# Low halves of the weight blocks: an accumulating GpSimd DMA in place of a VectorE subtraction

## The chip, the cores and the metric

The kernel runs on one core of one Trainium2 chip. A core has a matrix engine (TensorE, PE in the profile), a vector engine (VectorE, DVE), an activation engine (ScalarE, ACT), a general engine (GpSimd, POOL) and a queue that issues plain transfers (SyncE, SP). The profile counts the loading of matmul weights apart, as PEld. Sixteen DMA engines move data for all queues. The metric is the device time of one execution in microseconds (us), the median of several runs. One execution has been recorded by the hardware profiler, and all rows of the trace come from it.

## The reference

The reference is one layer of a decoder trunk on 512 tokens of width 1024, with 16 learned tokens put in front (528 positions in all). Its steps:

```
u    = rmsnorm(h) * w
proj = u @ w_in                       # pool | z | x,B,C | dt | two gates
y_pool = pool_mixer(proj.pool) @ w_pool_up        # causal means over 2, 4, 8, 16 positions
xbc  = silu(causal_conv4(proj.xBC));  dt = softplus(proj.dt + dt_bias)
y    = ssd_chunked(x, dt, -exp(a_log), B, C) + x * d_skip   # Mamba-2, chunks of 128, 8 groups of 4 heads
y_ssd = (group_rmsnorm(y * silu(z)) * norm_w) @ w_ssd_out
h    = h + (gate_pool * y_pool + gate_ssd * y_ssd) @ w_o
h    = h + relu(rmsnorm(h) @ w_ff1)**2 @ w_ff2
out  = rmsnorm(h)[16:]
```

Everything is float32, and nearly all of the arithmetic is products with weight matrices.

## The kernel before, in words

**Products in three parts.** TensorE takes the operands in a rounded form of float32 (F32R in the code). To keep precision, every operand is split in two: a high half, which is the value rounded to that form, and a low half, which is the value minus its high half. A product is then three matmuls: high by high, high by low, low by high (`mm3`, lines 88 to 93, and `proj_step`, lines 139 to 146, where the low half of the weights is read by line 146).

**Weight blocks.** The host lays all weights out as blocks of 128 partitions by 1024 float32 (512 KB), in the order in which the program uses them. `block()` (lines 76 to 79) takes the next one: SP loads it into `raw` (line 72), ScalarE copies it, rounded, into `whi` (line 73), and VectorE subtracts the high half from the raw block and writes `wlo` (line 74). There are three buffers for `raw` and four each for `whi` and `wlo` (lines 66 to 68 and 55). A buffer of `whi` or `wlo` is free again when TensorE has read it for the last time. A block is 48 matmuls of some 260 columns, or 24 of 512.

**Stages.** The first stage works on the input as it arrives: the time-step weights, then eight blocks for group 0 and three gates (lines 520 to 525). Then comes a loop over the eight groups of the state-space part (line 562): `ssd(g)` does the group's own arithmetic on ScalarE, VectorE and TensorE, and is woven with `group_proj(g + 1)`, which runs the projections of the next group from four blocks `px`, at times one gate, and two blocks `pz`, and with parts of the output projection (`pso`, `psp`). Then come the pooling branch (`pp`, `psl`, `pg`), the gates and merge (`pgs`, `pup`), the output product (`wo`), and last the feed-forward part (`pf`).

**The feed-forward part.** It uses a recursive scheme (Strassen and Winograd) on quarters of the second weight matrix. In each of seven rounds, four blocks of the first matrix (`pf`, lines 867 to 887 and 911 to 944) are mixed with seven products of the second (`alpha`, `p`, `q`, lines 956 to 958). The operands of the latter are sums of quarters, made by GpSimd (line 967, 128x1024 each) and then split by ScalarE and VectorE (`split`, lines 713 to 719, into the same four buffers of `whi` and `wlo`, where the profile calls them `shi` and `slo`).

**What sets the order.** Each engine runs its instructions in one fixed order. That order is made when the program is built: a planner goes through the program with its own costs and, on each engine, takes what is ready by then, the earlier in the program first. On the chip an engine stops at an instruction whose operands are not there, and what is queued behind it waits as well. GpSimd is one such queue: it holds the loads of `abc` (line 391, one for each group, from a buffer in DRAM), of `ht` and `fw` (lines 754 and 755), and the sums of line 967.

Of the kernel before, what the change touches and what calls it, by code (L numbers as in the profile page):

```python
# [11 lines left out]
AF = mybir.ActivationFunctionType  # L12
ALU = mybir.AluOpType
# [36 lines left out]
def kernel(ctx: ExitStack, tc, xT, x, w, vec, fnw, out):  # L50
    nc = tc.nc
    act, dve, pe, pool = nc.scalar, nc.vector, nc.tensor, nc.gpsimd
# [6 lines left out]


    nblk = [0]

    def block_tiles():
        b = nblk[0]
        nblk[0] += 1
        return (b, wp.tile([P, 1024], F32, tag="raw", name=f"raw{b}", bufs=3),
                wp.tile([P, 1024], F32R, tag="whi", name=f"whi{b}"),
                wp.tile([P, 1024], F32R, tag="wlo", name=f"wlo{b}"))

    def block_part(t, c):  # L70
        b, raw, hi, lo = t
        nc.sync.dma_start(raw[:, c], w[b, :, c])
        act.copy(hi[:, c], raw[:, c])  # L73
        dve.tensor_tensor(lo[:, c], raw[:, c], hi[:, c].bitcast(F32), op=ALU.subtract)  # L74

    def block():
        t = block_tiles()
        block_part(t, slice(0, 1024))
        return t[2:]

    def units():

        while True:
            hi, lo = block()
            for j in range(NK):
                yield hi[:, j * P : (j + 1) * P], lo[:, j * P : (j + 1) * P]
# [94 lines left out]
    b, raw, hi, lo = wdt  # L181
# [156 lines left out]
    def group_tiles(g):  # L338
        xc = gc.tile([P, 2, L], F32, tag="xc", name=f"xc{g}")
        bt = gc.tile([P, L], F32, tag="bt", name=f"bt{g}")  # L340
        ct = gc.tile([P, SEQ], F32, tag="ct", name=f"ct{g}")
        zt = gc.tile([P, 2, SEQ], F32, tag="zt", name=f"zt{g}", bufs=1)
        return xc, bt, ct, zt
# [7 lines left out]
    def group_proj(g, cur, gate=None):  # L351

        first = g == 0
        xc, bt, ct, zt = cur
        for dst, t, skip in ((bt, 16 + g, 0), (ct, 24 + g, NM - 4), (xc[:, 0, :], 2 * g, 0),
                             (xc[:, 1, :], 2 * g + 1, 0)):
            if first and dst is bt:
                view = viewB
            else:
                runs, view = wide(psum2(f"px{g}_{t}"), skip)  # L360
                proj(runs, block(), X if first else U)
            conv(dst, first_raw(t, view, skip) if first else view, t)
            yield
        if gate is not None:
            gate_pool(gate)
            yield
        ps = psum2(f"pz{g}")
        for i in range(2):
            proj(narrow(ps[:, i * SEQ : (i + 1) * SEQ]), block(), X if first else U)
        zf = zt.rearrange("p i t -> p (i t)")  # L370
        if first:
            dve.tensor_tensor(zt, ps.rearrange("p (i t) -> p i t", i=2),
                              rsb[:, NM:].unsqueeze(1).to_broadcast([P, 2, SEQ]), op=ALU.mult)
            act.activation(zf, zf, AF.Silu)
        else:
            act.activation(zf, ps, AF.Silu)
        yield
# [125 lines left out]
    def weave(a, b, n):  # L503

        end = object()
        a = [a]
        while a or b:
            for s in [a] + [b] * n:
                if s and next(s[0], end) is end:
                    s.pop(0)  # L510
# [33 lines left out]
    def out_half():  # L544
        for dd in range(4):
            ps = psum2(f"pso{dd}")
            for i in range(2):
                ssd_out(2 * dd + i, ps[:, i * SEQ : (i + 1) * SEQ], range(8))
                act.copy(acc[2 * dd + i], ps[:, i * SEQ : (i + 1) * SEQ])
                yield  # L550

    def out_part():

        un = units()
        for d in range(NK):
            ps = psum2(f"psp{d}")[:, :SEQ]
            for k in range(8, 14):
                mm3(ps, next(un), ys[k], k == 8, k == 13)
            dve.tensor_tensor(acc[d], acc[d], ps, op=ALU.add)
            yield  # L560

    for g in range(G):
        nxt = group_tiles(g + 1) if g + 1 < G else None
        fill = [group_proj(g + 1, nxt, GATE_AT.get(g))] if nxt else [out_part()]
        if g == 4:
            fill = [out_half()] + fill
        weave(ssd(g, cur), fill, 2 if g == 4 else 1)
        cur = nxt
# [638 lines left out]
```

## Time and profile before

| | us |
|---|---|
| median of 2 runs | 1025.61 (1025.49 to 1025.72) |
| span of the profiled execution, first to last instruction | 1023.3 |
| what lies around the span, to the median | 2.3 |
| TensorE busy | 1014.6 |
| VectorE busy | 730.3 |
| ScalarE busy | 552.5 |
| GpSimd busy | 88.7 |

The time of the profiled execution itself is not given beside its span; the 2.3 us is the median less the span. Busy times are those of one engine and overlap. Issuing a DMA is not counted as busy for SP and ScalarE. Where a row of a group stands, its columns are the line, the engine, the operation with the tiles that it writes and reads, the shapes, the count, then busy time and the mean length of one in ns, then the idle time of that engine ahead of these instructions and what ended it. In a timeline, the columns are start, length, engine, line, operation, and in brackets the idle time before it.

### The profile page before, as it was taken

How to read it: one execution, taken by the hardware profiler on the slowest of the kernel's cores; microseconds unless marked ns; L12 is line 12 of the kernel's file. 1: busy time of each engine (PE TensorE's matmuls, PEld its weight loads, DVE VectorE, ACT ScalarE, POOL GpSimd, SP SyncE). 2: the span in 40 equal slices, each digit the busy share in tenths (PEclk: the TensorE clock that was granted, in tenths of full speed). 3: DMA queues.
4: the chain of work that ended last, by engine and by line, in shares of the span. 5: the costliest groups of instructions: out<-in, count | busy, mean ns of one | idle time of the engine just before them, and what ended most of it. 6: DMA issues, size and time to landing. Idle time of an engine off the chain costs nothing.

```text
span 1023.3 us, 14063 instructions
## 1 busy us (share of the span) xinstructions
PE 1014.6 (99%) x5697; PEld 876.7 (86%) x5697; DVE 730.3 (71%) x954; ACT 552.5 (54%) x728; POOL 88.7 (9%) x52
## 2 busy tenths in 40 slices
PE   9999999999999999999999999999999999999997
PEld 8889989998879898988899888888888888888886
DVE  7978788687746586978755457975777577666866
ACT  7775968586627339573244343474545355454444
POOL 0100000000000000000000001003040421413400
PEclk9999999999999999999999999999999999999999
DMA  7243051414332331414532333224323323334112
GB/s 237 72 160 103 21 166 38 148 46 141 102 101 86 103 104 42 145 41 141 189 102 84 103 104 120 86 91 156 103 69 122 120 83 113 95 102 124 42 42 83
DMA packets 29281, 105.63 MB, mean 103 GB/s; under 512 B 3296, under 2 KB 4256, under 8 KB 28192
## 3 DMA queue, kind: packets, MB, share of 16 engines
q1 hardware_dynamic: 26496, 92.75, 28.7%
q0 software_dynamic: 2000, 11.08, 3.0%
q8 instruction: 45, 0.74, 0.3%
q10 hardware_dynamic: 720, 0.91, 0.3%
q14 instruction: 20, 0.16, 0.1%
HBM read 102.55 MB, written 2.16 MB: 102 GB/s over the span
## 4 chain that ended last, share of the span: by engine, by line
PE 96%; DVE 2%; ACT 0%; DMA 0%; issue 0%; SPq 0%; ACTq 0%
PE px L143 6%; PE px L144 6%; PE pf L92 6%; PE pf L91 6%; PE px L146 6%; PE pf L90 6%; PE alpha L956 3%; PE alpha L957 3%; PE alpha L958 3%; PE pz L143 3%; PE pz L146 3%; PE pz L144 3%; PE py L470 2%; PE pso L90 2%; PE pp L144 2%; PE pp L146 2%
## 5 line engine op out<-in xcount | busy, mean ns | idle before, releaser
L73 ACT CAST whi<-raw 128x1024 fp32r<-128x1024 f32 (+1 forms) x131 | 135.7, 1043 | 220.0 <-PE pf L91 55.8
L74 DVE TENSOR_TENSOR wlo<-raw,whi 128x1024 fp32r<-128x1024 f32 (+1 forms) x131 | 163.6, 1251 | 112.6 <-ACT whi L73 105.3
L143 PE MATMUL px<-uh,whi 128*128 128x264 f32 (+1 forms) x448 | 121.2, 290 | 0.7 <-DVE ct L334 0.7
L144 PE MATMUL px<-ul,whi 128*128 128x264 f32 (+1 forms) x448 | 118.9, 285 | 0.0
L90 PE MATMUL pf<-vh,whi 128*128 128x512 f32 x256 | 99.8, 390 | 0.0
L92 PE MATMUL pf<-vh,wlo 128*128 128x512 f32 x256 | 99.6, 389 | 0.0
L91 PE MATMUL pf<-vl,whi 128*128 128x512 f32 x256 | 99.6, 389 | 0.0
L146 PE MATMUL px<-uh,wlo 128*128 128x264 f32 (+1 forms) x448 | 90.8, 284 | 0.0
L143 PEld LDWEIGHTS px<-uh,whi 128*128 128x128 f32 x448 | 84.6, 189 | 2.8 <-issue 2.6
L144 PEld LDWEIGHTS px<-ul,whi 128*128 128x128 f32 x448 | 84.8, 189 | 0.3
L718 DVE TENSOR_TENSOR slo<-b,shi 128x1024 fp32r<-128x1024 f32 x35 | 49.1, 1403 | 31.6 <-ACT shi L717 31.6
L146 PEld LDWEIGHTS px<-uh,wlo 128*128 128x128 f32 x448 | 69.4, 188 | 0.3 <-issue 0.3
L717 ACT CAST shi<-b 128x1024 fp32r<-128x1024 f32 x35 | 36.8, 1050 | 47.2 <-PE pf L91 36.4
L91 PEld LDWEIGHTS pf<-vl,whi 128*128 128x128 f32 x256 | 48.1, 188 | 10.0
L90 PEld LDWEIGHTS pf<-vh,whi 128*128 128x128 f32 x256 | 48.1, 188 | 9.9
L92 PEld LDWEIGHTS pf<-vh,wlo 128*128 128x128 f32 x256 | 48.1, 188 | 9.9
L967 POOL TENSOR_TENSOR b<-b,b 128x1024 f32<-128x1024 f32 x14 | 35.7, 2548 | 238.3 <-DVE slo L718 238.3
L956 PE MATMUL alpha<-shi,hh 128*128 128x512 f32 x140 | 54.6, 390 | 0.0
L957 PE MATMUL alpha<-slo,hh 128*128 128x512 f32 x140 | 54.5, 389 | 0.0
L958 PE MATMUL alpha<-shi,hl 128*128 128x512 f32 x140 | 54.5, 389 | 0.0
L783 DVE TENSOR_TENSOR ht<-ht,alpha 128x1024 f32<-128x1024 f32 x35 | 42.5, 1214 | 10.9 <-PE alpha L958 10.9
L143 PE MATMUL pz<-uh,whi 128*128 128x512 f32 x112 | 44.0, 393 | 0.0
(412 smaller groups left out, 2513.7 us busy)
## 6 DMA issues: line engine op xcount, KB each, us to landing
raw<-in_w SPq DMA_DIRECT2D x129, 512.0 KB, 3.6
b<-in_w SPq DMA_DIRECT2D x28, 512.0 KB, 3.6
abc<-acs_d POOLq DMA_DIRECT2D x8, 1024.0 KB, 7.2
wob<-in_w SPq DMA_DIRECT2D x8, 512.0 KB, 4.6
xt<-in_xT SPq DMA_DIRECT2D x8, 264.0 KB, 5.6
ht<-in_x POOLq DMA_DIRECT2D x4, 512.0 KB, 6.7
w<-in_w SPq DMA_DIRECT2D x4, 512.0 KB, 3.6
out_dram<-out SPq DMA_DIRECT2D x4, 320.0 KB, 2.4
```

Of the source, the lines that this page charges most:

```text
L73: act.copy(hi[:, c], raw[:, c])
L74: dve.tensor_tensor(lo[:, c], raw[:, c], hi[:, c].bitcast(F32), op=ALU.subtract)
L90: pe.matmul(ps, ah, bh, start=first, stop=False)
L91: pe.matmul(ps, ah, bl, start=False, stop=False)
L92: pe.matmul(ps, al, bh, start=False, stop=last)
L143: pe.matmul(o, wh, rhs[0][k][:, c], start=k == 0, stop=False)
L144: pe.matmul(o, wh, rhs[1][k][:, c], start=False, stop=False)
L146: pe.matmul(o, wl, rhs[0][k][:, c], start=False, stop=k == NK - 1)
L718: dve.tensor_tensor(lo, src, hi.bitcast(F32), op=ALU.subtract)
L956: pe.matmul(ps[t], a[0], wh[:, cs], start=f, stop=False, skip_group_check=True)
L957: pe.matmul(ps[t], a[0], wl[:, cs], start=False, stop=False, skip_group_check=True)
L958: pe.matmul(ps[t], a[1], wh[:, cs], start=False, stop=l, skip_group_check=True)
```

## The change

From the loop over the groups on, a block's low half is made in another way. ScalarE writes the negated rounded block into `wlo` (its own scaling by -1 on the way), and a DMA that GpSimd issues reads the block from DRAM once more and adds it to what stands in `wlo`. ScalarE then makes the high half as before. The first-stage blocks, and all operands that go through `split`, stay as they were.

```
+    low_by_dma = [False]
...
     def block():
         t = block_tiles()
-        block_part(t, slice(0, 1024))
+        if not low_by_dma[0]:
+            block_part(t, slice(0, 1024))
+            return t[2:]
+        b, raw, hi, lo = t
+        nc.sync.dma_start(raw, w[b])
+        act.activation(lo, raw, AF.Copy, scale=-1.0)
+        nc.gpsimd.dma_start(lo, w[b], accum_op=ALU.add)
+        act.copy(hi, raw)
         return t[2:]
...
+    low_by_dma[0] = True
     for g in range(G):
         nxt = group_tiles(g + 1) if g + 1 < G else None
```

## The prediction

> **What bounds the kernel now.** First the page: busy times, then the engine shares of the chain that ended last.
>
> ```profile
> span 1023.3 us, 14063 instructions
> PE 1014.6 (99%) x5697; PEld 876.7 (86%) x5697; DVE 730.3 (71%) x954; ACT 552.5 (54%) x728; POOL 88.7 (9%) x52
> ...
> PE 96%; DVE 2%; ACT 0%; DMA 0%; issue 0%; SPq 0%; ACTq 0%
> ```
>
> TensorE is busy for 1014.6 of 1023.3 us, and the chain is 96% TensorE. It idles 8.7 us in all, so an edit that relieves only the other engines can win no more than that, 0.8%. What the change can do is lose: it puts a transfer between ScalarE's write and TensorE's first read of a low half. So two lengths decide: the room that a block's low half has today, and the time the transfer takes. Next, the groups by line, with shapes kept apart, and the view of the tile `wlo`, for who makes and who reads it.
>
> ```profile
> L74 DVE TENSOR_TENSOR wlo<-raw,whi 128x1024 fp32r<-128x1024 f32 x129 | 162.2, 1260 | 112.6 <-ACT whi L73 105.3 <-PE po L464 7.3
> L73 ACT CAST whi<-raw 128x1024 fp32r<-128x1024 f32 x129 | 134.4, 1049 | 220.0 <-PE pf L91 55.8 <-PE px L144 33.8 <-issue 32.6
> L146 PE MATMUL px<-uh,wlo x448: 278/284/391, 68.8 to 429.8; 128*128 128x264 f32 x113, 128*128 128x258 f32 x37
> L92 PE MATMUL pf<-vh,wlo x256: 389/389/398, 687.4 to 983.9; 128*128 128x512 f32 x128
> ```
>
> 129 whole blocks are made; 8 belong to the first stage, so 121 change. Their low half is ready 2.3 us after ScalarE starts (1.049 + 1.260), if VectorE is free. ScalarE's idle time ahead of L73 ends mostly with a matmul (`PE pf L91`, `PE px L144`): it waits for TensorE to give a buffer back, so the block can't start earlier.
>
> **The room.** I paired each of the 121 blocks, in program order, with the first matmul that reads its low half, and call "room" the time from the end of ScalarE's cast to the start of that matmul. The shortest are of two kinds. In the group loop ScalarE has one long run at a group's start, and the casts come only after it; four timeline pieces of ScalarE and TensorE (cast, then first reader):
>
> ```profile
> 265.45 1.03 ACT L73 CAST whi<-raw 128x1024 fp32r<-128x1024 f32 x1
> ...
> 269.05 0.58 PE L92 MATMUL pso<-yh,wlo 128*128 128x512 f32 x1
> ...
> 166.64 1.03 ACT L73 CAST whi<-raw 128x1024 fp32r<-128x1024 f32 x1
> ...
> 171.76 0.40 PE L146 MATMUL px<-uh,wlo 128*128 128x258 f32 x2
> ...
> 403.62 1.98 ACT L73 CAST whi<-raw 128x1024 fp32r<-128x1024 f32 x2
> ...
> 408.74 0.40 PE L146 MATMUL px<-uh,wlo 128*128 128x258 f32 x2
> ...
> 634.56 1.06 ACT L73 CAST whi<-raw 128x1024 fp32r<-128x1024 f32 x1 [0.18 <-PE pgs L144]
> ...
> 640.49 0.39 PE L92 MATMUL pup<-yph,wlo 128*128 128x512 f32 x1
> ```
>
> Rooms of 2.6, 4.1, 4.1 (the first of two casts ends near 404.65) and 4.9 us. The second kind recurs in each of the seven feed-forward rounds; here one round on ScalarE, GpSimd and TensorE:
>
> ```profile
> 755.68 1.06 ACT L73 CAST whi<-raw 128x1024 fp32r<-128x1024 f32 x1 [0.74 <-PE alpha L958]
> 761.85 1.05 ACT L73 CAST whi<-raw 128x1024 fp32r<-128x1024 f32 x1
> 769.06 1.05 ACT L73 CAST whi<-raw 128x1024 fp32r<-128x1024 f32 x1 [4.12 <-PE pf L91]
> ...
> 755.12 2.41 POOL L967 TENSOR_TENSOR b<-b,b 128x1024 f32<-128x1024 f32 x1 [33.09 <-DVE slo L718]
> 757.61 3.25 POOL L967 TENSOR_TENSOR t<-b,b 128x1024 f32<-128x1024 f32 x1
> 760.82 2.40 POOL L967 TENSOR_TENSOR b<-b,b 128x1024 f32<-128x1024 f32 x1
> ...
> 764.10 0.39 PE L92 MATMUL pf<-vh,wlo 128*128 128x512 f32 x1
> ...
> 772.26 0.39 PE L92 MATMUL pf<-vh,wlo 128*128 128x512 f32 x1
> ...
> 780.42 0.39 PE L92 MATMUL pf<-vh,wlo 128*128 128x512 f32 x1
> ```
>
> Rooms of 7.4, 9.4 and 10.3 us (the round's fourth block has 10.3 too). But the first block's cast ends at 756.74, while GpSimd is inside a sum. If its DMA is queued between the first sum and the second, it goes out at 757.53 and 6.6 us are left; if after the second, at 760.86, and 3.2 are left. By this pairing, 4 of 121 rooms are under 5 us, 7 under 6.7, 14 under 8, 25 under 10 and 50 under 13.4; the median is 15.0.
>
> **The transfer, "L".** No row of this trace shows an accumulating DMA. The nearest ones, from the DMA issues, the queues, and the view of line 391:
>
> ```profile
> raw<-in_w SPq DMA_DIRECT2D x129, 512.0 KB, 3.6
> abc<-acs_d POOLq DMA_DIRECT2D x8, 1024.0 KB, 7.2
> ht<-in_x POOLq DMA_DIRECT2D x4, 512.0 KB, 6.7
> fw<-in_fnw POOLq DMA_DIRECT2D x1, 512.0 KB, 9.8
> q1 hardware_dynamic: 26496, 92.75, 28.7%
> L391 POOL DMA_DIRECT2D abc<-acs_d x8: 527/530/566, 50.4 to 424.6; - x8
> DMA to landing us min/median/max: 4.9/7.2/8.4
> ```
>
> Lower bound: 3.6 us, a plain block on SP's queue. Upper bound: 13.4, two of GpSimd's 512 KB loads (6.7) one after the other, for reading the low half and then writing it. I take 6.7: the only 512 KB loads of the same queue, sent in a burst, which makes them slow, against an addition that must also read its target, which those need not. That `abc` moves 1 MB in 7.2 at the median speaks for the same number, since reading block and target is 1 MB too.
>
> [...]
>
> **The change part by part.**
> - *Removed:* 121 VectorE subtractions, 121 x 1.260 = 152 us. Worth nothing while TensorE is at 99%.
> - *Added on ScalarE:* 121 writes of 1.05 us (as L73), 127 us, and each high half comes 1.05 later. Two windows show the cover:
>
> ```profile
> 140.00:188.00 48.00, 48.00 (x333) 43.34 (x332) 36.80 (x57) 35.05 (x45) 0.00 (x0) 1.00 0.32 100
> 755.00:796.00 41.00, 41.00 (x182) 33.95 (x181) 27.80 (x23) 19.19 (x21) 11.43 (x5) 1.00 0.33 103
> ```
>
>   (columns: window, length, then busy time of PE, PEld, DVE, ACT, POOL, the clock, DMA share, GB/s). A group of 48 us has 35.05 of ScalarE and gets 7 x 1.05 = 7.4 more: 42.4, or 88%. It fits, in the time that ScalarE waits for buffers today, and VectorE's 8.8 us less (7 x 1.260) shortens its other waits. I cost it at nothing; without that cover it is up to 7.4 us a group. A feed-forward round goes from 19.19 to 23.4 of 41: covered.
> - *Moved:* SP's reloads of `raw` wait today for VectorE's subtraction (in the queue's waits, `SPq L72 <- DVE wlo L74`); now for ScalarE's second copy, at about the same time. Nothing.
> - *Added on GpSimd:* 121 issues of 0.53 us, 64 us on an engine with 88.7 busy: covered. But each waits for its ScalarE write, and queued behind it are the loads of `abc` (one a group) and the sums (four a round), for which `split` and then TensorE wait. As the planner orders by its own time, such a wait is short where its times are right; the sums then slip by 0.5 us or so. Nothing, with the queue's effect on the DMA itself counted above.
> - *Added on the DMA engines:* by the q1 row a 512 KB block takes 28.7% x 16 x 1023.3 us / 92.75 MB x 0.524 MB = 26.5 us of engine time, 1.66 us on all sixteen. Reading block and target for 121 blocks is 2 x 121 x 1.66 = 402 us; on a mean share of 0.32 (first window) that makes some 0.7. It fits, and delays raw loads at times; I count it in L.
> - *The wait that is added:* TensorE's, for L less the room, wherever that is positive. A matmul that waits moves all later ones, and buffers come free later by the same amount, so that waits of different blocks add up.
>
> Summed over the 121 rooms, with the feed-forward DMAs between the sums or behind them:
>
> | L, us | waits, between / behind |
> |---|---|
> | 3.6 | 5 / 19 |
> | 4.9 | 10 / 30 |
> | 6.7 | 21 / 49 |
> | 9.8 | 72 / 100 |
> | 13.4 | 222 / 250 |
>
> At 6.7 that is 11 us in the group loop and 9.5 or 38 after it. I take the middle, 35 us, as nothing tells where the planner puts the DMA. The profiled span becomes 1023.3 + 35 = 1058 us; the median of the runs shown is 2.3 above the span, so the **forecast is 1060 us**, 3.4% slower.
>
> **The rivals.**
> 1. *The transfer hides.* L is 4.9 or less, the DMAs go out between the sums, and TensorE waits 5 to 10 us, less what VectorE's relief gives back of the 8.7: 1024 to 1036. For it: the median room of 15 us and the 4.9 of the quickest `abc`; against it: rooms of 2.6 to 4.9 us, which even that doesn't fit. It decides below L = 5; at 20 us of waiting (L of 5 to 6.6, by the order) it is past the 2% that a measurement of this kernel tells from no change (1046).
> 2. *The addition is slow.* L is 9.8 or more, through element-wise work or two passes, or DMAs that queue behind each other: 25 rooms of 121 are too short, the second to fourth blocks of each round among them. 1098 at 9.8 between the sums, 1276 at 13.4 behind them. [...] For it: nothing in the trace shows an addition, and the 9.8 of `fw`.
> 3. *ScalarE becomes the bound of the group loop.* Seven groups are lengthened by 7.4 us each, 52 us: 1077. Against it: 88% after the change; for it: a fixed order that leaves little of the rest usable.
> 4. *Faster by over 2%* would need 20 us of TensorE's time; it idles 8.7.
>
> That the change doesn't do what it says isn't a case: every later block goes through the new lines.
>
> **How the numbers follow.** Forecast (L from 5 to 9, 1035 to 1090): 0.37. First rival 0.28, second 0.27, third 0.06, fourth 0.02. Of the forecast's share some 0.05 lies under 1046. So slower by over 2%: 0.32 + 0.27 + 0.06 = 0.65; within 2%: 0.28 + 0.05 = 0.33; faster: 0.02. The range goes from 1027 (waits of 3.6's size, half given back) to 1220, where L is about 12.5; it leaves out the best of the first rival and the worst of the second.
>
> **What would show it.** VectorE's busy time falls to about 578 us, ScalarE's rises to about 680. The landing of the new DMA gives L. TensorE's idle time names a DMA `wlo<-in_w` as releaser, some 3 us at the start of each group and 0 to 4 at the first block of each round. Wrong would be: an L outside 5 to 9; a planner that moves TensorE's order so that other work fills the waits; or a GpSimd queue in which a DMA stands far ahead of its block's write and holds up the sums.

## The result and the profile after

The changed kernel takes 1070.32 us (1069.32 to 1071.31, two runs) against 1025.61. The ratio is 1.0437, with a 95% interval of 1.0406 to 1.0467: slower by 4.4%. The forecast was 1060 us.

The page of the changed kernel first: the busy times, the granted clock in 40 slices, and the queue of the new DMA.

```profile
span 1069.6 us, 14301 instructions
...
PE 1028.6 (96%) x5697; PEld 886.7 (83%) x5697; DVE 595.7 (56%) x833; ACT 660.8 (62%) x849; POOL 180.1 (17%) x173
...
PEclk9999899999999999999999999899999999999999
...
q0 software_dynamic: 19424, 74.52, 36.1%
```

The profiled span grew by 46.3 us, in two parts. TensorE's **idle time** rose from 8.7 to 1069.6 - 1028.6 = 41.0 us, by 32.3. Its **busy time** for the same 5697 matmuls rose by 14.0 us. The first part is named by the view of the waits, limited to TensorE (what waited, for what; total us, times, longest):

```profile
PE px L154 <- DMA wlo<-in_w: 14.8, 4, 4.0
PE pf L100 <- DMA wlo<-in_w: 10.7, 6, 4.4
PE pup L100 <- DMA wlo<-in_w: 4.6, 1, 4.6
PE pso L100 <- DMA wlo<-in_w: 2.4, 1, 2.4
```

Together 32.5 us in 12 waits, all for the new DMA. So 12 blocks of 121 are late, and nothing else adds to the idle time. The second part shows in the clock row, where two slices are an 8: TensorE ran some stretches at half clock, each beginning within one of these waits or right behind it. Windows of 3.41 us show it (start and end; length; busy time of PE, PEld, DVE, ACT, POOL with their instructions; granted clock; DMA share, in which a packet counts where it starts, so that it can pass 1; GB/s):

```profile
120.29:123.70 3.41, 1.35 (x10) 1.08 (x8) 3.41 (x7) 3.41 (x5) 0.84 (x1) 1.00 0.84 229
123.70:127.11 3.41, 1.46 (x7) 1.47 (x8) 3.27 (x4) 3.38 (x5) 0.85 (x1) 0.50 1.05 240
127.11:130.53 3.42, 3.42 (x17) 3.42 (x17) 1.26 (x3) 1.52 (x2) 0.84 (x1) 0.50 1.05 277
...
178.31:181.73 3.42, 0.13 (x1) 0.13 (x2) 3.28 (x7) 1.70 (x2) 0.84 (x1) 1.00 1.05 259
181.73:185.14 3.41, 3.41 (x17) 3.41 (x18) 1.07 (x3) 3.28 (x3) 0.85 (x1) 0.50 1.05 273
185.14:188.55 3.41, 3.41 (x30) 3.41 (x30) 0.00 (x0) 0.65 (x1) 0.00 (x0) 1.00 1.06 275
```

At half clock 17 matmuls fill a window, at full clock 30. There are six such stretches, four of 3.41 and two of 6.83 us. The sum of the windows that cover just these (and the run's last 3.8 us, in which TensorE has nothing to do):

```profile
sum 31.11, PE 24.63 PEld 22.57 DVE 8.06 ACT 14.98 POOL 4.24; mean PE 3.52 PEld 3.22 DVE 1.15 ACT 2.14 POOL 0.61
```

TensorE was busy for 24.63 us at half clock. If that work takes half as long at full clock, it lost 12.3 of the 14.0 us (an estimate). Of the rest, 0.9 also shows in the first experiment below, which has no such stretch; what the rest comes of stays open.

The new transfer itself, by the issues of line 85 and by the landing of each tile:

```profile
L85 POOL DMA_DIRECT2D wlo<-in_w x121: 834/855/915, 51.7 to 1017.0; - x121
...
DMA to landing us min/median/max: 5.3/7.3/12.1
...
raw<-in_w SPq DMA_DIRECT2D x129, 512.0 KB, 5.7
```

It lands after 7.3 us at the median. An issue takes 0.855 us, and the plain loads of `raw` on the other queue now land after 5.7 us instead of 3.6.

**A group's start.** The timeline around 175 us, on ScalarE, GpSimd and TensorE (start, length, engine, line, operation, idle time before it):

```profile
173.29 1.04 ACT L84 ACTIVATE wlo<-raw 128x1024 fp32r<-128x1024 f32 x1
...
174.64 0.84 POOL L85 DMA_DIRECT2D wlo<-in_w  x1 [20.49 <-PE px L154]
...
177.67 0.38 PE L472 MATMUL po<-ct,st 128*128 128x128 f32 x2
181.60 0.70 PE L154 MATMUL px<-uh,wlo 128*128 128x258 f32 x2 [3.55 <-DMA wlo<-in_w]
```

ScalarE's write ends at 174.33, the DMA goes out 0.3 us later, and 7.0 us after that TensorE goes on. It had nothing else in its order for 3.6 us. The two matmuls that then start take 0.70 us, where the same two took 0.40 in the kernel before (at 171.76).

**A block that wasn't tight before.** The first late block, at 121 us, had a room of 21.3 us in the kernel before (from 99.89, the end of the cast, to 121.22):

```profile
98.84 1.05 ACT L73 CAST whi<-raw 128x1024 fp32r<-128x1024 f32 x1 [1.53 <-PE px L144]
...
121.22 0.28 PE L146 MATMUL px<-uh,wlo 128*128 128x258 f32 x1
```

In the changed kernel the high half of this block is still cast at that place, but ScalarE's order has the write of the low half 19 us later, behind the whole run of the group's own work, and TensorE waits 4.0 us:

```profile
98.69 1.06 ACT L86 CAST whi<-raw 128x1024 fp32r<-128x1024 f32 x1
...
116.75 1.06 ACT L444 ACTIVATE abc<-abc 128x1024 f32<-128x1024 f32 x1
117.72 1.04 ACT L84 ACTIVATE wlo<-raw 128x1024 fp32r<-128x1024 f32 x1
...
125.65 0.58 PE L154 MATMUL px<-uh,wlo 128*128 128x258 f32 x1 [4.00 <-DMA wlo<-in_w]
```

**A feed-forward round**, on GpSimd and TensorE:

```profile
789.90 2.39 POOL L976 TENSOR_TENSOR t<-b,b 128x1024 f32<-128x1024 f32 x1
792.25 0.86 POOL L85 DMA_DIRECT2D wlo<-in_w  x1
...
797.55 0.50 PE L100 MATMUL pf<-vh,wlo 128*128 128x512 f32 x1 [1.02 <-DMA wlo<-in_w]
```

The DMA of the round's first block stands behind the second sum. It lands after 5.3 us here, and TensorE waits for 1.0 us. Four more rounds do the same. In the last one the DMA goes out at 1002.06, only 1.0 us before TensorE needs the block, and the wait is 4.4 us.

### The profile page after: what moved, and what is told of

It is laid out like the page before. It is cut to its first block, busy times and chain, and to the rows that moved or that the text cites. A ratio compares the mean times of both kernels' runs of the same rounds, so it can differ in the third digit from the quotient of the medians.

```text
span 1069.6 us, 14301 instructions
## 1 busy us (share of the span) xinstructions
PE 1028.6 (96%) x5697; PEld 886.7 (83%) x5697; DVE 595.7 (56%) x833; ACT 660.8 (62%) x849; POOL 180.1 (17%) x173
## 3 DMA queue, kind: packets, MB, share of 16 engines
q0 software_dynamic: 19424, 74.52, 36.1%
## 4 chain that ended last, share of the span: by engine, by line
PE 64%; issue 24%; DMA 7%; POOL 2%; DVE 2%; ACT 0%; POOLq 0%; ACTq 0%
DMA wlo<-in_w 7%; PE px L151 5%; PE px L154 5%; PE px L152 5%; PE pf L100 3%; PE pf L98 3%; PE pf L99 2%; PE py L478 2%; POOL b L976 2%; PE pp L154 1%; PE pp L152 1%; PE pp L151 1%; PE pgs L151 1%; PE pgs L152 1%; PE pgs L154 1%
## 5 line engine op out<-in xcount | busy, mean ns | idle before, releaser
L86 ACT CAST whi<-raw 128x1024 fp32r<-128x1024 f32 x121 | 126.7, 1047 | 186.8 <-PE pf L99 69.6
L85 POOL DMA_DIRECT2D wlo<-in_w x121 | 103.3, 854 | 628.0 <-ACT wlo L84 493.2
L84 ACT ACTIVATE wlo<-raw 128x1024 fp32r<-128x1024 f32 x121 | 127.8, 1056 | 15.0 <-DMA raw<-in_w 7.3
L151 PE MATMUL px<-uh,whi 128*128 128x264 f32 (+1 forms) x448 | 124.8, 297 | 0.0
L152 PE MATMUL px<-ul,whi 128*128 128x264 f32 (+1 forms) x448 | 122.2, 292 | 0.0
L100 PE MATMUL pf<-vh,wlo 128*128 128x512 f32 x256 | 100.9, 394 | 10.7 <-DMA wlo<-in_w 10.7
L154 PE MATMUL px<-uh,wlo 128*128 128x264 f32 (+1 forms) x448 | 93.6, 292 | 14.8 <-DMA wlo<-in_w 14.8
L151 PEld LDWEIGHTS px<-uh,whi 128*128 128x128 f32 x448 | 88.1, 197 | 2.2 <-issue 1.9
L152 PEld LDWEIGHTS px<-ul,whi 128*128 128x128 f32 x448 | 88.2, 197 | 0.3
L154 PEld LDWEIGHTS px<-uh,wlo 128*128 128x128 f32 x448 | 72.0, 194 | 15.6 <-DMA wlo<-in_w 15.6
```

What stands on the lines that cost most here:

```text
L84: act.activation(lo, raw, AF.Copy, scale=-1.0)
L85: nc.gpsimd.dma_start(lo, w[b], accum_op=ALU.add)
L86: act.copy(hi, raw)
L100: pe.matmul(ps, al, bh, start=False, stop=last)
L151: pe.matmul(o, wh, rhs[0][k][:, c], start=k == 0, stop=False)
L152: pe.matmul(o, wh, rhs[1][k][:, c], start=False, stop=False)
```

## The experiments

The kernel before took 1025.0 to 1025.1 us on the chips of these runs. All ratios are against it.

### Only the late blocks made by VectorE

The 12 late blocks, and one that was nearly late, take the old path; 108 keep the DMA.

```
+    BY_VECTOR = (16, 23, 30, 37, 38, 58, 97, 108, 112, 116, 120, 124, 127)
...
         t = block_tiles()
-        if not low_by_dma[0]:
+        made[0] += 1
+        if not low_by_dma[0] or made[0] in BY_VECTOR:
             block_part(t, slice(0, 1024))
```

> The thirteen blocks for which TensorE waited in the changed kernel (the first of each group, one pso, one pup, the first of each feed-forward round) get their low half from VectorE again; the other 108 keep the DMA. Theory (TensorE waits only where the room is shorter than the landing time, and its half clock follows from these waits): the 36 us of waits and the 14 us at half clock go, 1024 to 1032 us. Rival (the load itself costs: 108 more ScalarE writes, 108 more transfers beside the raw loads): little changes, 1058 to 1070 us. A third way: other blocks become late in their place, 1040 to 1055 us.

1026.89 us (1026.53 to 1029.0), ratio 1.0022 (1.0011 to 1.0033). TensorE's busy time on the page, and the one wait for a DMA that is left:

```profile
PE 1015.5 (99%) x5697; PEld 876.0 (85%) x5697; DVE 611.6 (60%) x846; ACT 648.1 (63%) x836; POOL 174.4 (17%) x160
...
PE pf L103 <- DMA wlo<-in_w: 0.7, 1, 0.7
```

108 accumulating DMAs and 108 more writes on ScalarE cost nearly nothing. The mean granted clock of the profiled run is 0.999, as in the kernel before; the changed kernel had 0.985. So the loss comes from a few late blocks, and not from the load on ScalarE, GpSimd or the DMA engines at large.

The same with only the seven blocks ahead of the feed-forward part:

```
-    BY_VECTOR = (16, 23, 30, 37, 38, 58, 97, 108, 112, 116, 120, 124, 127)
+    BY_VECTOR = (16, 23, 30, 37, 38, 58, 97)
```

> As the run with thirteen VectorE blocks, but only the seven outside the feed-forward part (the first blocks of the groups, two pso, one pup); the six late blocks of the feed-forward rounds keep the DMA. Theory: the waits and half clock of the group loop go (24 us and 12 us), those of the rounds stay (12 us and 2 us): 1036 to 1042 us. Rival (the gain of the thirteen came from the rounds): 1055 to 1062 us.

1037.96 us (1037.16 to 1038.76), ratio 1.0126 (1.0096 to 1.0155). The waits that are left on TensorE:

```profile
PE pf L103 <- DMA wlo<-in_w: 10.2, 6, 4.4
```

So the rounds cost 1037.96 - 1026.89 = 11.1 us, and what lies before them 1070.32 - 1037.96 = 32.4. The latter agrees with the trace of the changed kernel: there the waits of those blocks are 14.8 + 4.6 + 2.4 = 21.8 us, and the half clock behind them, by the same estimate, (24.63 - 3.42) / 2 = 10.6, which makes 32.4.

### Low halves read last

In each block the matmuls with the low half of the weights come after all others, which gives the DMA more room.

```
-            proj_step(outs, k, wblk, rhs)
+            wh = wblk[0][:, k * P : (k + 1) * P]
+            for o, c in outs:
+                pe.matmul(o, wh, rhs[0][k][:, c], start=k == 0, stop=False)
+                pe.matmul(o, wh, rhs[1][k][:, c], start=False, stop=False)
+        for k in range(NK):
+            wl = wblk[1][:, k * P : (k + 1) * P]
+            for o, c in outs:
+                pe.matmul(o, wl, rhs[0][k][:, c], start=False, stop=k == NK - 1)
...
```

(and the same order in the loops over `mm3`).

> All 121 blocks keep the DMA; within a block TensorE runs all matmuls with the high half of the weights first and those with the low half last, in proj, ssd_out, the merge's products and ff1_part. The first read of a low half comes some 3.6 us later (two thirds of a block of 5.5 us). Theory of the room: waits of up to 4.8 us shrink to at most 1.2 us, no half clock is left, 1025 to 1031 us. Rival (ScalarE or the transfers are the bound): 1060 to 1072 us, since the work of every engine is the same.

1043.53 us (1042.57 to 1045.05), ratio 1.0184 (1.0167 to 1.0201): 26.8 of the 44.7 us go, where nearly all of it was expected to. TensorE's timeline at a group's start, then two rows of its waits:

```profile
172.16 0.39 PE L167 MATMUL px<-uh,whi 128*128 128x258 f32 x1 [0.86 <-ACT whi L86]
...
178.51 0.56 PE L172 MATMUL px<-uh,wlo 128*128 128x258 f32 x2 [2.27 <-DMA wlo<-in_w]
```

```profile
PE px L172 <- DMA wlo<-in_w: 6.0, 3, 2.3
PE pst L471 <- ACT btm L424: 2.0, 1, 2.0
```

The block's low half is still late by 2.3 us, though the high-half matmuls run ahead of it. And TensorE now waits for ScalarE as well: for the high half, which ScalarE writes second (0.86), and for tiles of the group's own work (2.0 for `btm`, 1.8 for `acc`). TensorE's own order differs from the changed kernel's, too. In all it idles 24.9 us, and half clock is left in two stretches of 3.41 us.

As a control, the kernel before with its low halves last:

> The kernel before the change with the low-half matmuls last in each block, as a control for the run with lows last on the changed kernel. Theory (rooms are long enough before the change, so that more of them is worth nothing): 1023 to 1027 us. If the other order in itself costs time through the planner's order: 1030 to 1045 us, and what the changed kernel gave with lows last holds that cost.

1023.56 us (1022.68 to 1024.36), ratio 0.9985 (0.9973 to 0.9996). Again, in more rounds:

> The kernel before the change with the low-half matmuls last in each block, timed in more rounds: 1022.5 to 1024.5 us, 0.1 to 0.2% under the kernel before, if the 1.4 us seen once are the order's own; 1024.5 to 1026 us if they were scatter.

1023.2 us (1022.64 to 1024.11), ratio 0.9982 (0.9973 to 0.9991). So this order alone is worth 0.2%, with VectorE making every low half. This version beats both kernels. And both edits together, VectorE for 13 blocks and the low halves last:

> VectorE for the thirteen late blocks, the DMA for the other 108, and the low-half matmuls last in each block. If lows last adds room where it is short and nothing else: 1022 to 1025 us, at or a little under the kernel before. If ScalarE's extra writes hold up high halves, as in the changed kernel with lows last, where TensorE waited for the high half: 1026 to 1035 us.

1032.98 us (1030.82 to 1033.31), ratio 1.0071 (1.0058 to 1.0083), worse than either of its two parts, the 13 blocks (1026.89) and the order without the DMA (1023.2). No wait for a DMA is left; TensorE's largest in total is for VectorE, and two of 1.1 and 1.9 us are for ScalarE:

```profile
PE po L489 <- DVE st L481: 3.7, 8, 0.9
```

By these waits, it is ScalarE's and VectorE's other work that comes late in this order. The profiled run of this kernel took 1030.82 us; why its other runs are some 2 us slower stays open.

### The same DMA without the addition

```
-        nc.gpsimd.dma_start(lo, w[b], accum_op=ALU.add)
+        nc.gpsimd.dma_start(lo, w[b])
```

> The DMA copies the block over the low half without adding (the addition is left out, so that the low half is the block itself); all else, the wait for ScalarE's write too, stays. If the addition costs a second read of 512 KB (about 1.7 us on sixteen engines), the landing time falls from 7.3 to some 5.6 us at the median, the thirteen waits lose 1 to 1.7 us each and some half clock goes: 1035 to 1050 us. If the addition itself is slow, it falls to 4 to 5 us: 1026 to 1036 us. If the addition is free and the rest is GpSimd's issue and the queue: 7 us and 1066 to 1072 us.

1037.94 us (1037.67 to 1038.2), ratio 1.0125 (1.0105 to 1.0145). Its page's row of the queue, and its issues and landing by line 85:

```profile
q0 software_dynamic: 19424, 74.52, 21.1%
...
L85 POOL DMA_DIRECT2D wlo<-in_w x121: 530/530/857, 51.5 to 983.9; - x121
...
DMA to landing us min/median/max: 3.7/4.6/8.9
```

Against 7.3 at the median and 0.855 to issue: the addition is 2.7 us of the landing and 0.32 us of the issue. The same queue in the kernel before, which has no block on it:

```profile
q0 software_dynamic: 2000, 11.08, 3.0%
```

With that taken off (3.0% of 1023.3 is 30.7 us), a block takes (21.1% x 1036.5 - 30.7) / 121 = 1.55 us of all sixteen engines as a copy and (36.1% x 1069.6 - 30.7) / 121 = 2.94 as an addition, 1.9 times as much. The 1.4 us between the two are near the 1.7 at which the expectation put a second read of 512 KB; no row shows that read by itself. The landing grew by 2.7 us, more than the engine time did. Without the addition the `raw` loads land after 3.7 us again. So the addition made both transfers slower, and 32 of the 45 us hang on it. The rest is a transfer that even as a copy is too long for the tightest rooms: TensorE still waits 9.5 us for it, at seven blocks, and runs one stretch of 6.83 us at half clock.

### ScalarE's extra write alone

```
         act.activation(lo, raw, AF.Copy, scale=-1.0)
-        nc.gpsimd.dma_start(lo, w[b], accum_op=ALU.add)
         act.copy(hi, raw)
+        dve.tensor_tensor(lo, raw, hi.bitcast(F32), op=ALU.subtract)
```

> No DMA: VectorE makes the low half by subtraction as before, but ScalarE still writes the negated block into it first (which VectorE then overwrites). ScalarE's load is that of the changed kernel. Theory (ScalarE's 127 us are covered): low halves come 1.05 us later than before, rooms allow it, 1024 to 1030 us. Rival (ScalarE is the bound of the group loop): up to 7.4 us a group, 1050 to 1077 us.

1031.55 us (1031.54 to 1031.56), ratio 1.0063 (1.0043 to 1.0083). The window of a group that the prediction weighed, and VectorE's wait for the extra write:

```profile
140.00:188.00 48.00, 46.24 (x315) 41.42 (x315) 35.74 (x56) 37.51 (x49) 0.00 (x0) 1.00 0.28 90
...
DVE wlo L86 <- ACT wlo L84: 67.5, 32, 5.7
```

ScalarE's writes cost 6 us where VectorE isn't relieved, a little more than expected. That is far from the 52 us by which they would have made ScalarE the bound of the group loop: it is busy for 37.51 us of 48, with six of the extra writes in this window.

### The high half first on ScalarE

```
         nc.sync.dma_start(raw, w[b])
+        act.copy(hi, raw)
         act.activation(lo, raw, AF.Copy, scale=-1.0)
         nc.gpsimd.dma_start(lo, w[b], accum_op=ALU.add)
-        act.copy(hi, raw)
```

> The changed kernel with ScalarE's two writes swapped: the high half first, then the negated one, so that each DMA goes out about 1.05 us later. Theory of the room: each of the thirteen waits grows by about 1 us and some blocks that just fitted (rooms 0.1 to 0.5 us over the landing time) join them, 13 to 18 us more, and perhaps a half clock more: 1083 to 1095 us. Rival (the landing time doesn't matter by itself): 1066 to 1074 us.

1080.84 us (1079.82 to 1081.86), ratio 1.0544 (1.0513 to 1.0575), between the two expectations. TensorE idles 44.4 us, only 3.4 more. At three of the four late group starts the room fell by 0.7 to 0.9 us, but the transfer took 0.2 to 0.6 us less; in the rounds the DMA stands behind a sum anyway, and nothing changed. The other 5.1 us are busy time: four of its seven stretches at half clock lasted 6.83 us, where the changed kernel had two of six.

### Zero matmuls in the gaps

To take the half clock away and leave the waits, 30 matmuls that add zeros are put behind the first high-half matmuls of five late blocks (16, 23, 30, 58, 97).

```
+        if k == 0 and made[0] in FILL:
+            for _ in range(30):
+                pe.matmul(outs[0][0][:, :256], wh, zero_r, start=False, stop=False)
```

> The changed kernel, with 30 matmuls of 256 zero columns (0.11 us each, 3.3 us in all, they add zero to the result) put behind the first high-half matmuls of five blocks, in the places where TensorE waited 3.7 to 4.8 us and then ran at half clock for 3.4 to 6.8 us (four group starts and one pup). The landing times stay. Theory (the half clock comes of TensorE standing still for more than some 3 us, and costs 12 us in these five places): the waits are filled, the half clock goes there, TensorE's busy time apart from the filling falls by some 12 us, 1056 to 1062 us. Rival (the half clock has another cause, or the filling isn't hidden by the wait): half clock as before, 1070 to 1087 us.

1065.44 us (1064.88 to 1066.01), ratio 1.0394 (1.0364 to 1.0424): 4.9 us less than the changed kernel, where more was expected. TensorE's timeline at the first of these blocks, then the windows around two late blocks that were not filled:

```profile
122.09 3.68 PE L163 MATMUL px<-zero_r,whi 128*128 128x256 f32 x30
126.42 0.51 PE L165 MATMUL px<-uh,wlo 128*128 128x258 f32 x2 [0.65 <-DMA wlo<-in_w]
126.77 0.28 PE L159 MATMUL px<-uh,whi 128*128 128x258 f32 x1
```

```profile
281.97:285.38 3.41, 1.32 (x6) 1.10 (x7) 2.54 (x7) 1.87 (x2) 0.84 (x1) 1.00 0.98 256
285.38:288.79 3.41, 3.41 (x10) 2.64 (x9) 0.00 (x0) 1.99 (x2) 0.85 (x1) 0.50 1.02 267
...
995.36:998.77 3.41, 0.19 (x1) 0.00 (x0) 3.41 (x3) 0.87 (x1) 3.04 (x3) 1.00 0.78 132
998.77:1002.18 3.41, 2.20 (x5) 1.83 (x6) 0.42 (x1) 0.00 (x0) 0.15 (x1) 0.50 0.92 147
1002.18:1005.60 3.42, 3.42 (x9) 2.68 (x9) 0.00 (x0) 0.00 (x0) 0.00 (x0) 0.50 0.53 182
```

At all five filled places the clock stays full (the mean granted clock is 0.994, against 0.985; at the first place it is 1.00 from 121.54 to 128.37 us), and there the matmuls behind the gap take 0.28 us at once. So the half clock follows from TensorE standing still. The time lost to it, estimated as above, falls from 12.3 us to (3.41 + 2.20 + 3.42) / 2 = 4.5. That is 7.8 us, of which the span kept 6.5; where the other 1.3 went stays open. Two places that were not filled got worse: the wait near 285 us now brings half clock, and the one at the end brings 6.83 us of it instead of 3.41.

**Why the same wait does both.** In each trace the half-clock stretches start whole multiples of 3.413 us apart: in the changed kernel 123.70 and 181.73 are 17 of them apart, 123.70 and 1007.75 are 259 (884.05 / 259 = 3.413). So I cut nine traces (the changed kernel's and those of the experiments with the DMA or the extra write) into such windows, from the phase that each trace shows, and looked at each window's busy time. Of windows at full clock, all 19 that half clock follows before the run's end have TensorE busy for 1.61 us or less, and none that is followed by full clock has less than 1.50 (in the changed kernel alone, six with 0.00 to 1.35 us and none with less than 1.91). The closest two, of the experiment with the high half first and of the one without the addition:

```profile
290.39:293.81 3.42, 1.61 (x18) 1.14 (x16) 2.26 (x6) 3.42 (x4) 1.69 (x2) 1.00 1.04 237
```

```profile
971.49:974.90 3.41, 1.50 (x7) 0.93 (x5) 3.41 (x3) 2.18 (x3) 2.76 (x3) 1.00 0.41 118
```

The first is followed by half clock, the second isn't. In the changed kernel, two windows at half clock are followed by another, with TensorE busy for 1.46 and 2.68 us of them; behind the other six, with 3.41 or 3.42 us, the clock is full again. The wait at 286.5 us in the changed kernel (2.4 us) is as long as the one near 285 us in the filled kernel (2.3 us), but falls on both sides of a boundary:

```profile
284.13:287.54 3.41, 2.41 (x12) 1.77 (x10) 3.20 (x4) 3.41 (x5) 1.07 (x2) 1.00 0.76 112
287.54:290.96 3.42, 2.05 (x9) 1.71 (x10) 1.88 (x5) 1.58 (x3) 0.84 (x1) 1.00 1.03 272
```

The two parts idle 1.00 and 1.37 us, and the clock stays full; in the filled kernel 2.09 us lie in one window, and it halves. This is read off the traces and was not tried by moving a wait against the boundaries.

The least that brought half clock in these traces was 1.8 us idle in one window (3.42 less 1.61).

## Why the prediction was right, and where it was wrong

**Right: the direction, the place, and, by luck, the sum of the waits.** 35 us were forecast and 32.3 measured, all for the new DMA, as named. They fall at four group starts, at one `pso` and one `pup` block and at the first blocks of six rounds: eleven blocks whose rooms the prediction had found short, and one more. The expected sign at each group's start, some 3 us of idle time, came at four of them, with 3.5 to 4.0 us. The first experiment shows that these waits, with what follows from them, are nearly the whole loss.

**The sum came out of two errors that cancel.** In the group loop, 11 us were counted, and it is 14.8 + 2.4 = 17.2. After it, the middle was 24 (9.5 or 38), and it is 4.6 + 10.7 = 15.3.
- *In the group loop*, the rooms were taken from the trace before, as if ScalarE's order stayed. It didn't: the block at 121 us was tight only after the change, for 4.0 us. At the other three late group starts the room from ScalarE's write to TensorE's need is 3.5 to 3.7 us, where it was 4.1 to 5.7, and the transfer goes out 0.3 us behind the write. At the `pso` block it is longer, 3.3 against 2.6. The `pup` block, behind the loop, kept its room, but its transfer took 9.1 us.
- *In the rounds*, the planner put the DMA behind the second sum, the bad one of the two cases. But the transfer there took 5.3 to 5.7 us, not 6.7, and the second sum 2.39 instead of 3.25. Five waits became 1.0 to 1.5 instead of 3.5. In the last round, 4.4.

**The transfer time, L.** Taken: 6.7, from GpSimd's plain loads (the four of `ht`, issued within 1.6 us, land after 5.2, 5.9, 7.5 and 8.7 us, the later the slower). At the six late blocks ahead of the rounds it was 5.4 to 9.1, five of them at 7.0 or less; the median of all is 7.3. The bounds of 3.6 and 13.4 held. What those loads didn't show is that the addition nearly doubles the engine time (1.9 times). That it reads its target was taken as given in the argument; no run shows it by itself.

**Wrong by omission: the half clock.** The step "a matmul that waits moves all later ones" made a wait cost its own length. Here every wait of 3.5 us or more left TensorE at half clock for one or two windows, and by the estimate above that cost 12.3 us more. It is most of what TensorE's busy time grew by, and without that growth of 14.0 us the changed kernel would have come in some 4 us under the forecast, at 1056.

**Costs put at nothing.** ScalarE's 127 us: TensorE's waits in the changed kernel name no tile of ScalarE's, but the 4.0 us at 121 us come from a late write of ScalarE's; why its order has that write so late stays open. With VectorE not relieved, the writes cost 6 us. The issues on GpSimd: 0.855 us instead of 0.53, 103 us in all, covered. The reloads of `raw`: they land 2.1 us later, and TensorE doesn't wait for them. VectorE's relief was indeed worth nothing. Its busy time is 595.7 us, not 578, and ScalarE's 660.8, not 680: the prediction summed lengths, and where an instruction starts before its neighbour ends, busy time counts the overlap once. On neither does the end depend.

**The rivals.** That the transfer hides fell: twelve blocks don't hide it, and no transfer of the changed kernel landed within its 4.9 us (the quickest took 5.3). It holds for 109 of 121, though, and with the twelve and one more made by VectorE again the kernel is 0.2% slower than the one before. That the addition is slow (9.8 or more) fell as a median; single landings reach 12.1 us, where the room is long. ScalarE as the bound fell by its own experiment.

## What to carry to other kernels

When a transfer is put between two engines of a kernel that is full on a third, count the rooms one by one, and in the order that the planner makes with the change: a mean says nothing, since here 12 of 121 blocks made the whole loss. Price a wait of TensorE by more than its length: by these traces a wait under 1.8 us (3.41 less 1.61) that has its window to itself costs its own length. One above some 3.8 us leaves at least 1.91 us idle (3.41 less 1.50) in one window wherever it falls, and every window of that kind in the nine traces brought half clock, which cost an estimated 1.7 to 3.0 us more at each place in the changed kernel. Between the two it depends on where the wait falls. If a move to a slower path is wanted, leave the few tight items on the fast one.

## What the runs showed of the hardware

- In the nine traces, the stretches at half clock (0.50) start whole multiples of 3.413 us apart. Cut into such windows, the clock halved behind every window at full clock with TensorE busy for less than 1.50 us, behind none with more than 1.61, and between the two it did both. In the changed kernel it stayed half behind windows with 1.46 and 2.68 us of work and was full again behind those with 3.41 or more.
- A DMA that adds 512 KB from DRAM to what stands in the tile took 2.94 us of all sixteen DMA engines against 1.55 as a copy, landed after 7.3 us against 4.6, and took GpSimd 0.855 us to issue against 0.53.
- It also slowed the plain loads of another queue beside it, from 3.6 to 5.7 us; a copy in its place left them at 3.7.
- Running the high-half matmuls of a block first and the low-half ones after them made the kernel before faster by 0.2% (1023.2 us against 1025.14). Why was not examined.
